# Layer 0's ramp in a two-layer encoder step: the second triangular inverse in other memory, the first read back behind its writing, fourteen products earlier

## The chip, the cores and the metric

The kernel runs on one core of a Trainium2 chip. The core has five engines with queues of their own: TensorE (PE, matrix products; its weight loads are listed as PEld), VectorE (DVE), ScalarE (ACT), GpSimd (POOL) and SyncE (SP, which here issues nearly every DMA). Semaphores order them against each other; within one engine, and within SP's DMA queue, work is issued in program order. The metric is the device time of one execution in microseconds (us), of which less is better.

## The reference

A streaming encoder trunk of two layers takes 512 prompt rows and 32 sample rows of width 1024. Each layer normalizes, projects once, runs a token mixer and a memory cross-attention, gates the result with SiLU, projects out and adds the residual. Layer 0's mixer is RWKV-7, a recurrence over a 64 x 64 state per head, 24 heads:

```python
def step(S, inp):
    r_t, k_t, v_t, w_t, kk_t, a_t = inp
    sa = jnp.einsum('bhvk,bhk->bhv', S, -kk_t)
    S = (S * w_t[:, :, None, :] + sa[..., None] * (kk_t * a_t)[:, :, None, :]
         + v_t[..., None] * k_t[:, :, None, :])
    return S, jnp.einsum('bhvk,bhk->bhv', S, r_t)
```

Layer 1's mixer is differential attention. Everything is float32.

## The kernel before

The 544 token rows lie as columns. A projection of 128 output columns is a *block* of 48 products: the weights are split into a high and a low part, and `ps_g` gathers, for each of 8 slices of the depth, high times `hh`, high times `hl` and low times `hh`, in two halves of 272 columns. `load` brings a block's weights in two pieces of 256 KB (`raw`, five buffers); ACT casts each to `whi` and DVE makes `wlo`, once for each piece. `stream` loads the weights of a block two blocks ahead and puts the casts off to places between products (`some`).

The recurrence is done in chunks of 64 tokens, for two heads (a *pair*) at once; there are 12 pairs. For a pair, `rw_prep` (a generator, taken a step at a time) makes decayed keys and the chunks' triangular matrices `at` and, for the sample rows, `ats`. The diagonal 32 x 32 blocks have to be inverted:

- at its end `rw_prep` writes these blocks to a DRAM scratch `sc1` (`sc<-at`, `sc<-ats` in the profile, which leaves numbers out of names);
- `rw_invert` ("inv") reads the scratch into `m3` three times, so that 102 partitions hold 34 blocks and three column classes, sets `u3` to the identity `ui` and does 31 steps of two POOL instructions (`tm`, `u`);
- `rw_back` ("back") writes `u3` to a second scratch `sc2`, and `rw_at` ("at") reads that back into `at` and `ats`;
- `rw_merge` ("mrg") makes from the two inverted blocks of a 64 x 64 matrix its off-diagonal block: DVE transposes (`t1b`), PE multiplies (`ps_w1`), ACT copies (`wm`), PE multiplies (`ps_w2`), ACT copies into `at`. In the profile both products are `ps_w`.

`m3` and `u3` have one buffer each, so an inverse can begin only when the one before has been written out. Then `rw_values` ("val") makes `ps_v`, and `rw_chain` takes the state through eight chunks in 23 hops between PE, ACT and DVE (`ps_c`, `sv`, `SB`, `avz`).

The order of every engine's work in layer 0 is fixed by the program: `go(kind, pair)` emits a step and `fill(n)` emits n products of the stream. The ramp (lines 1395 to 1426) takes pair 0's preparation with `FILL0`, pair 1's with `FILL1`, eleven steps of pair 2's with `FILL2`, and pair 0's merge and values with `FILL3`. In the ramp "back 0" stands ahead of `FILL2`'s loop, and "at 0" and "inv 1" at its fourth place:

```python
go("back", 0)
for k, n in enumerate(FILL2):
    go("prep", 2)
    if k == 2:
        go("rsq", 2)
    if k == 3:
        go("at", 0)
        go("inv", 1)
    fill(n)
```

Then the main loop takes, for each pair, the 23 chain hops with a table `PLAN` of steps for other pairs between them; `each[pr]` products are spread over the hops by their due times (144 for pair 0). The step `load_up`, in `rw_prep`, loads `up` for the pair after when DVE's `uz` has used the one before. `sg`, two tiles of 544 columns, hold gates from pair 1's loop on. `gsq` is a tile for squares in `rw_finish`, first used in pair 1's loop.

Of the kernel before, what the change touches and what calls it, by code (L numbers as in the profile page):

```python
# [9 lines left out]
F32 = mybir.dt.float32  # L10
# [7 lines left out]
P = 128  # L18
# [4 lines left out]
T = TP + TS  # L23
TH = T // 2
MIXW = 1536
NPAIR = MIXW // P
# [12 lines left out]
SGB = 2  # L39
# [38 lines left out]

FILL0 = [4, 4, 8, 2, 6, 2, 2, 2, 6, 2, 18, 4, 4, 2, 2, 0, 8, 12, 4, 8, 14, 10, 6, 14, 2, 0, 2, 2, 2, 2, 2, 2]
FILL1 = [6, 14, 12, 2, 4, 2, 2, 2, 8, 0, 10, 0, 2, 8, 8, 6, 4, 6, 6, 8, 18, 12, 8, 10, 0, 0, 0, 0, 4]  # L80
FILL2 = [4, 6, 12, 2, 2, 0, 4, 0, 6, 2, 2]
FILL3 = [16, 0, 2, 6]

OUT_ORDER = [0, 1, 2, 3, 4, 5, 6, 7, 8, 9, 10, 12, 13, 14, 15, 11]
# [3 lines left out]
NCL = 3  # L88
NBLK = 34
# [16 lines left out]
class Trunk:  # L106
# [600 lines left out]
    def rw_invert(self, st):  # L707

        nc, p, sc1 = self.nc, self.rb, st["sc1"]
        m3 = p.tile([NCL * NBLK, 32, 32], F32, tag="m3", name="m3", bufs=1)  # L710
        for q in range(NCL):
            self.se.dma_start(m3[q * 32 : q * 32 + 32], sc1[:32])
            self.se.dma_start(m3[96 + 2 * q : 98 + 2 * q], sc1[32:])
        st["u3"] = u3 = p.tile([NCL * NBLK, self.nr, 32], F32, tag="u3", name="u3", bufs=1)
        nc.gpsimd.tensor_copy(u3[:], self.ui[:])
        tm = p.tile([NCL * NBLK, self.nr, 32], F32, tag="tm", name="tm", bufs=1)
        for kx in range(31):
            n = kx // NCL + 1
            wd = 31 - kx
            sh = [NCL * NBLK, n, wd]  # L720
            nc.gpsimd.tensor_tensor(tm[:, :n, :wd], u3[:, :n, kx : kx + 1].to_broadcast(sh),  # L721
                                    m3[:, kx : kx + 1, kx + 1 :].to_broadcast(sh), ALU.mult)
            nc.gpsimd.tensor_tensor(u3[:, :n, kx + 1 :], u3[:, :n, kx + 1 :], tm[:, :n, :wd], ALU.add)  # L723

    def rw_back(self, st):

        u3 = st["u3"]
        st["sc2"] = sc2 = self.dp.tile([NBLK, 32, 32], F32, tag="sc2", name="sc2", bufs=2)
        for q in range(NCL):
            n = len(range(q, 32, NCL))  # L730
            for b, o, m in ((0, q * 32, 32), (32, 96 + 2 * q, 2)):
                self.se.dma_start(sc2[b : b + m, q : 32 : NCL, :], u3[o : o + m, :n, :])

    def rw_at(self, st):

        at, ats, sc2 = st["at"], st["ats"], st["sc2"]
        for e in range(2):
            o = 64 if e == 0 else 0
            for b in range(2):
                n = (e * 2 + b) * 8  # L740
                u = slice(o + 32 * b, o + 32 * b + 32)
                self.se.dma_start(at[u, e, 1 - e].rearrange("p i h t -> p (i h) t")[:, :, 32 * b : 32 * b + 32],
                                  sc2[n : n + 8].rearrange("b s t -> s b t"))
        self.se.dma_start(ats[64:96, 1, :, :32], sc2[32:34].rearrange("h s t -> s h t"))

    def rw_merge(self, st):

# [508 lines left out]
    def layer0(self, mem):  # L1256
        nc, o = self.nc, self.o
# [5 lines left out]
        with ExitStack() as ctx:  # L1263
# [23 lines left out]
            def go(kind, pr):  # L1287

                if kind == "rsq":
                    self.rsqrt(self.r20[:], self.q20[:], self.rk0, "nt20")  # L1290
                elif 0 <= pr < NPAIR:
                    if kind in ("inv", "back", "at"):
                        {"inv": self.rw_invert, "back": self.rw_back, "at": self.rw_at}[kind](sts[pr])
                        return
                    if (kind, pr) not in run:
                        it = run[kind, pr] = self.rw_prep(sts[pr], rkv[pr]) if kind == "prep" else make[kind](sts[pr])
                        next(it)
                    next(run[kind, pr], None)


            blocks, each = [], [0] * NPAIR
# [84 lines left out]
            def fill(n, each=6):  # L1386

                while n > 0:
                    for _ in range(min(n, each)):
                        next(main)  # L1390
                    n -= each
                    self.some(LATER)
# [20 lines left out]
                nc.gpsimd.memset(t[:, 4, :], 0.0)  # L1413
            self.pads(self.zr[2])
            self.at.append(self.rb2.tile([P, 2, 2, 4, 2, 64], F32, name="at2"))
            go("back", 0)
            for k, n in enumerate(FILL2):
                go("prep", 2)
                if k == 2:
                    go("rsq", 2)  # L1420
                if k == 3:
                    go("at", 0)
                    go("inv", 1)
                fill(n)
            for kind, n in zip(("mrg", "mrg", "val", "mrg"), FILL3):
                go(kind, 0)
                fill(n)
            for pr in range(NPAIR):
                mplan = MPLAN.get(pr, ())
                took = [HOP + sum(us for x in y for kind, d, us, _ in x if 0 <= pr + d < NPAIR) for y in PLAN]  # L1430
                load = [HOPV[k % 3] + sum(us for x in y for kind, d, _, us in x if 0 <= pr + d < NPAIR) for k, y in enumerate(PLAN)]
                whole = sum(took) + MEMPE * len(mplan) / 12 + MAIN * each[pr]

                pace = [max(x, 1.4) for x in load] if each[pr] < 3 * 6 * KT else [1.0] * len(PLAN)
                due = [whole * sum(pace[:k]) / sum(pace) for k in range(len(PLAN) + 1)]
                room = (sum(load) + 2.3 * each[pr] / 48) / len(PLAN)
                t, left, spent = 0.0, each[pr], 0.0
                for k, y in enumerate(PLAN):
                    go("chain", pr)
                    t += HOP  # L1440
                    spent += HOPV[k % 3]
                    for half, x in enumerate(y):
                        for kind, d, us, vus in x:
                            if 0 <= pr + d < NPAIR and kind != "full":
                                go(kind, pr + d)
                                t += us
                                spent += vus
                        for at, h in mplan:
                            if at == k + half / 2:
                                if h not in mit:  # L1450
                                    mit[h] = self.mem_steps(mems[h], 0, h, self.ma)
                                    next(mit[h])
                                next(mit[h], None)
                                t += MEMPE / 12
                        if FULL not in x:
                            spent += self.some(room * (k + (half + 1) / 2) + 0.4 - spent)
                        while left and t + MAIN / 2 < (due[k + 1] if half else (due[k] + due[k + 1]) / 2):
                            next(main)
                            t += MAIN
                            left -= 1  # L1460
# [27 lines left out]
        with ExitStack() as ctx:  # L1488
            p = self.pool("wo0", 1, ctx=ctx)
# [64 lines left out]
            pr = [self.psc.tile([P, 512], F32, tag="c", name="ps_r") for _ in range(2)]  # L1554
            for i in range(5):
                n = P if i < 4 else TS
# [4 lines left out]
            for k in range(KT):  # L1561
                h = p.tile([P, T], F32, tag="hn", name="hn", bufs=HNB)
# [253 lines left out]
    def run(self):  # L1816
# [9 lines left out]
        nc = self.nc  # L1826
# [5 lines left out]
        self.hl = hp.tile([P, KT, T], F32R, name="hl")  # L1832
        self.wp = self.pool("w", 1)
        gp = self.pool("gate", 1)
        self.sg, self.gates = [gp.tile([P, T], F32, name=f"sg{i}") for i in range(SGB)], 0
        self.rctx = ExitStack()
        self.rb = self.pool("rwb", 1, ctx=self.rctx)
        self.zr = [self.rb.tile([P, ZW], F32, name=f"zr{i}") for i in range(2)]
# [49 lines left out]
```

## Time and profile before

| What | Value |
|---|---|
| Median of three runs | 1451.4 us (1451.32 to 1452.59) |
| The profiled execution | 1452.73 us, span 1451.0 us |
| Mean granted clock of TensorE | 0.986 |
| PE, DVE, ACT, POOL busy | 96%, 63%, 58%, 27% of the span |
| DMA | 139.2 MB, mean 96 GB/s |

A timeline row gives a start and a duration in us, the engine, the line, the operation and its tiles, and in brackets how long the engine was idle before it and what ended that. Rows of equal instructions are merged, with their count. Nearly all work goes through a helper at line 103, so rows are told apart by their tiles. SPq rows are DMA issues and not landings. A table of stretches gives, for each, the busy time of the engines with the number of instructions, the granted clock as a share of full speed, the DMA engines' busy share and GB/s.

### The profile page before, as it was taken

Reading aid. Unit: us, or ns where it says so; the run is one execution under the profiler, and the core shown is the slowest. Engines: PE = TensorE matmul, PEld = TensorE weight load, DVE = VectorE, ACT = ScalarE, POOL = GpSimd, SP = SyncE. Lnnn points to the kernel's source line nnn. Section 1 sums busy time; section 2 is a strip of 40 time slices with the busy share of each in tenths; the row PEclk is TensorE's granted clock in tenths of the full one; section 3 lists DMA queues with packets and bytes.
Section 4 is the critical chain, followed back from the end, with each engine's and each line's share of the span. In section 5 each row is a group of like instructions: output and inputs, shape, how many; then the busy total and the mean of one; then the engine's idle time right before and its main releaser. Section 6 shows DMA issues by size and latency. Waiting matters only on the chain.

```text
span 1451.0 us, 31979 instructions
## 1 busy us (share of the span) xinstructions
PE 1397.4 (96%) x11906; PEld 1318.0 (91%) x11906; DVE 919.9 (63%) x2337; ACT 835.6 (58%) x2293; POOL 388.2 (27%) x846
## 2 busy tenths in 40 slices
PE   6998899999999999899999999999999999999997
PEld 5997899999999998788899999999999999999997
DVE  6565667787777887575743566664465745657533
ACT  6664667667776777455543366653565546664322
POOL 2025676566866567500120030000000001000200
PEclk9998999999999999999999999999999999999999
DMA  6442123323223222232554473323323222332321
GB/s 217 124 135 73 27 62 92 81 73 78 63 78 96 69 73 66 77 91 84 174 157 131 132 201 103 84 75 92 113 69 95 80 84 81 89 98 67 97 88 70
DMA packets 266533, 139.20 MB, mean 96 GB/s; under 512 B 57657, under 2 KB 256578, under 8 KB 266378
## 3 DMA queue, kind: packets, MB, share of 16 engines
q1 hardware_dynamic: 266378, 137.16, 33.4%
q8 instruction: 94, 1.54, 0.5%
q14 instruction: 61, 0.50, 0.1%
HBM read 110.98 MB, written 22.78 MB: 92 GB/s over the span
## 4 chain that ended last, share of the span: by engine, by line
PE 80%; DVE 7%; ACT 6%; issue 2%; POOL 2%; DMA 2%; SPq 1%; DVEq 0%; ACTq 0%; POOLq 0%
PE ps_g L103 57%; PE ps_c L103 4%; PE ps_s L103 2%; PE ps_o L103 2%; PE ps_at L103 2%; PE ps_mm L103 1%; PE ps_v L103 1%; DVE wlo L103 1%; PE ps_mo L103 1%; SPq L103 1%; PE ps_aT L103 1%; POOL u L723 1%; PE ps_ss L103 1%; PE ps_yc L103 1%; POOL tm L721 1%
## 5 line engine op out<-in xcount | busy, mean ns | idle before, releaser
L103 PE MATMUL ps_g<-hh,wlo 128*128 128x272 f32 x1808 | 539.5, 298 | 1.4 <-DVE wlo L103 1.4
L103 PE MATMUL ps_g<-hh,whi 128*128 128x272 f32 x1808 | 538.8, 298 | 0.0
L103 PE MATMUL ps_g<-hl,whi 128*128 128x272 f32 x1808 | 533.5, 295 | 0.0
L103 DVE TENSOR_TENSOR wlo<-raw,whi 128x512 fp32r<-128x512 f32 x322 | 224.1, 709 | 199.7 <-ACT whi L103 195.7
L103 PEld LDWEIGHTS ps_g<-hh,wlo 128*128 128x128 f32 x1808 | 342.8, 190 | 5.8 <-DVE wlo L103 2.0
L103 PEld LDWEIGHTS ps_g<-hh,whi 128*128 128x128 f32 x1808 | 343.6, 190 | 4.1
L103 PEld LDWEIGHTS ps_g<-hl,whi 128*128 128x128 f32 x1808 | 343.2, 190 | 3.9 <-issue 0.6
L103 ACT CAST whi<-raw 128x512 fp32r<-128x512 f32 x322 | 195.0, 617 | 180.5 <-PE ps_g L103 103.6
L721 POOL TENSOR_TENSOR tm<-u,m 102x84 f32<-102x84 f32 (+23 forms) x372 | 158.0, 425 | 181.1 <-DMA m<-sc 152.9
L723 POOL TENSOR_TENSOR u<-u,tm 102x84 f32<-102x84 f32 (+23 forms) x372 | 159.4, 429 | 29.1
L103 PE MATMUL ps_g<-lo,whi 128*128 128x272 f32 x512 | 148.6, 290 | 2.1 <-DVE lo L103 1.9
L103 PE MATMUL ps_g<-hi,whi 128*128 128x272 f32 x512 | 149.5, 292 | 0.8 <-ACT hi L103 0.8
L103 PE MATMUL ps_g<-hi,wlo 128*128 128x272 f32 x512 | 148.7, 290 | 0.9 <-DVE wlo L103 0.9
L1162 POOL TENSOR_TENSOR lo<-og,hi 128x544 fp32r<-128x544 f32 x8 | 13.7, 1713 | 485.8 <-DVE og L103 350.6
L103 PEld LDWEIGHTS ps_g<-lo,whi 128*128 128x128 f32 x512 | 97.2, 190 | 2.9 <-DVE lo L103 2.4
L103 PEld LDWEIGHTS ps_g<-hi,whi 128*128 128x128 f32 x512 | 97.2, 190 | 1.0 <-ACT hi L103 1.0
L103 PEld LDWEIGHTS ps_g<-hi,wlo 128*128 128x128 f32 x512 | 97.1, 190 | 1.1 <-DVE wlo L103 1.1
L103 DVE SCALAR_TENSOR_TENSOR SB<-ps_c,dl,sd 64x64 f32<-64x64 f32 x168 | 47.4, 282 | 47.4 <-PE ps_c L103 42.1
L103 ACT COPY sv<-ps_c 64x64 f32<-64x64 f32 x192 | 39.3, 205 | 39.0 <-PE ps_c L103 37.2
L103 ACT ACTIVATE pt<-ps_s,snm 128x128 f32<-128x128 f32 (+3 forms) x96 | 50.7, 529 | 18.1 <-DVE snm L103 17.0
L103 ACT ACTIVATE sg<-ps_g 128x272 f32<-128x272 f32 x64 | 25.3, 395 | 59.8 <-PE ps_g L103 59.5
L103 ACT COPY raw<-ps_g 128x272 f32<-128x272 f32 x74 | 28.6, 386 | 32.5 <-PE ps_g L103 31.8
(366 smaller groups left out, 2600.6 us busy)
## 6 DMA issues: line engine op xcount, KB each, us to landing
raw<-in_rw_in_dram SPq DMA_DIRECT2D x114, 256.0 KB
raw<-in_df_in_dram SPq DMA_DIRECT2D x112, 256.0 KB
raw<-in_w_out_dram SPq DMA_DIRECT2D x64, 256.0 KB
m<-sc SPq DMA_DIRECT2D x36, 128.0 KB
oscr<-sg SPq DMA_DIRECT2D x16, 272.0 KB
lo<-oscr SPq DMA_DIRECT2D x16, 272.0 KB
raw<-in_w_mem_k_dram SPq DMA_DIRECT2D x16, 256.0 KB
raw<-in_w_mem_v_dram SPq DMA_DIRECT2D x16, 256.0 KB
```

The lines of the kernel that those rows point to most:

```text
L103: return lambda *a, **k: self.trunk.tie(self, issue(*a, **k))
L721: nc.gpsimd.tensor_tensor(tm[:, :n, :wd], u3[:, :n, kx : kx + 1].to_broadcast(sh), m3[:, kx : kx + 1, kx + 1 :].to_broadcast(sh), ALU.mult)
L723: nc.gpsimd.tensor_tensor(u3[:, :n, kx + 1 :], u3[:, :n, kx + 1 :], tm[:, :n, :wd], ALU.add)
L1162: (self.nc.gpsimd if g % 2 else self.ve).tensor_tensor(lo[:], t, hi[:].bitcast(F32), ALU.subtract)
```

## The change

- Pair 1's inverse (and no other) takes its input into the gates' memory, which is now one tile `sg2` of which `sg[0]` and `sg[1]` are halves, and its result into `gsq`'s tile (`u3r`). It shares no buffer but `tm` with pair 0's inverse.
- "inv 1", "back 0" and "at 0" now stand together, in this order, at the third place of `FILL2`'s loop. "back 0" so moves behind the load of `up` and behind inverse 1's reads on SP, and two weight pieces move from ahead of "at 0" to behind it.
- `sc2` becomes two scratch tiles, of 32 and of 2 blocks, for all pairs; `rw_back` writes the three pieces of the large one first, and each read in `rw_at` waits only for its own tile.
- `FILL2` has 13 entries instead of 11 and 54 products instead of 40. Two steps of pair 2's preparation go with them out of pair 0's part of the main loop, which has 130 products instead of 144.

```diff
-FILL2 = [4, 6, 12, 2, 2, 0, 4, 0, 6, 2, 2]
+FILL2 = [4, 6, 12, 2, 2, 0, 4, 0, 6, 2, 6, 4, 6]
...
     def rw_invert(self, st):
...
-        m3 = p.tile([NCL * NBLK, 32, 32], F32, tag="m3", name="m3", bufs=1)
+        if st["pr"] == 1:
+            m3 = self.sg2[: NCL * NBLK, :1024].rearrange("p (s t) -> p s t", t=32)
+            u3 = self.rk0.tile([P, 10, 64], F32, tag="gsq", name="u3r", bufs=1)
+            u3 = u3[: NCL * NBLK].rearrange("p a b -> p (a b)")[:, : self.nr * 32].rearrange("p (n t) -> p n t", t=32)
+        else:
+            m3 = p.tile([NCL * NBLK, 32, 32], F32, tag="m3", name="m3", bufs=1)[:]
+            u3 = p.tile([NCL * NBLK, self.nr, 32], F32, tag="u3", name="u3", bufs=1)[:]
...
     def rw_back(self, st):
...
-        st["sc2"] = sc2 = self.dp.tile([NBLK, 32, 32], F32, tag="sc2", name="sc2", bufs=2)
-        for q in range(NCL):
-            n = len(range(q, 32, NCL))
-            for b, o, m in ((0, q * 32, 32), (32, 96 + 2 * q, 2)):
-                self.se.dma_start(sc2[b : b + m, q : 32 : NCL, :], u3[o : o + m, :n, :])
+        st["sc2"] = [self.dp.tile([m, 32, 32], F32, tag=f"sc2{m}", name=f"sc2{m}", bufs=2) for m in (32, 2)]
+        for o, t in zip((0, 96), st["sc2"]):
+            m = t.shape[0]
+            for q in range(NCL):
+                n = len(range(q, 32, NCL))
+                self.se.dma_start(t[:, q : 32 : NCL, :], u3[o + q * m : o + q * m + m, :n, :])
...
-            go("back", 0)
             for k, n in enumerate(FILL2):
                 go("prep", 2)
                 if k == 2:
                     go("rsq", 2)
-                if k == 3:
+                    go("inv", 1)
+                    go("back", 0)
                     go("at", 0)
-                    go("inv", 1)
                 fill(n)
...
+            ready = len(FILL2) - 11
+            each[0] -= sum(map(sum, (FILL0, FILL1, FILL2, FILL3))) - 4 * 24 - 6 * 48
...
-                            if 0 <= pr + d < NPAIR and kind != "full":
+                            if kind == "prep" and pr == 0 and d == 2 and ready:
+                                ready -= 1
+                            elif 0 <= pr + d < NPAIR and kind != "full":
...
-        self.sg, self.gates = [gp.tile([P, T], F32, name=f"sg{i}") for i in range(SGB)], 0
+        self.sg2, self.gates = gp.tile([P, SGB * T], F32, name="sg2"), 0
+        self.sg = [self.sg2[:, i * T : i * T + T] for i in range(SGB)]
```

SP's queue after pair 1's blocks have been written to `sc1`, before (the last two writes of inverse 0, then `up`, weights, the read-back, and the first reads of inverse 1):

```order
L103 DMA sc2_1783<-u3_1265 32x10x32
L103 DMA sc2_1783<-u3_1265 2x10x32
L103 DMA up_1800<-in_rw_w_up_dram 64x128 x2
L103 DMA up_1800<-in_rw_a_up_dram 64x128 x2
L103 DMA raw_1840<-in_rw_in_dram 128x4x128
L103 DMA raw_1842<-in_rw_in_dram 128x4x128
L103 DMA at0_90<-sc2_1783 32x8x32 x4
L103 DMA ats_1232<-sc2_1783 32x2x32
L103 DMA m3_1862<-sc1_1740 32x1024
L103 DMA m3_1862<-sc1_1740 2x1024
```

The same place now, from the last reads of inverse 1 on (`up` and the four reads before them stand directly ahead):

```order
L103 DMA sg2_83<-sc1_1739 32x1024
L103 DMA sg2_83<-sc1_1739 2x1024
L103 DMA sc232_1892<-u3_1258 32x11x32 x2
L103 DMA sc232_1892<-u3_1258 32x10x32
L103 DMA sc22_1893<-u3_1258 2x11x32 x2
L103 DMA sc22_1893<-u3_1258 2x10x32
L103 DMA at0_89<-sc232_1892 32x8x32 x4
L103 DMA ats_1231<-sc22_1893 32x2x32
L103 DMA raw_1916<-in_rw_in_dram 128x4x128
L103 DMA raw_1918<-in_rw_in_dram 128x4x128
```

Inverse 1's reads and `up` have moved ahead of the writes of inverse 0, and the weights `raw` behind the read-back.

ACT's queue at the merge of pair 0, before (`raw01` is a projection's result, `wm` and `at0` the merge's copies, `avz` the values'):

```order
L103 COPY raw01_351<-ps_g_1846 128x272
L103 COPY wm_2017<-ps_w1_2000 32x256 x2
L103 COPY avz_94<-ps_v0_2020 64x2x128
L103 COPY at0_90<-ps_w2_2028 32x8x32 x2
L103 COPY raw01_351<-ps_g_1983 128x272
```

and now:

```order
L103 COPY raw01_350<-PC_257 128x1
L103 COPY wm_2049<-ps_w1_2032 32x256 x2
L103 COPY avz_93<-ps_v0_2052 64x2x128
L103 CAST whi_2019<-raw_1916 128x512
L103 COPY at0_89<-ps_w2_2062 32x8x32 x2
```

The second half of the projection's result is now copied ahead of the merge, and the cast of the first of the two weight pieces that SP loads behind the read-back stands ahead of the copy into `at0`. On PE the first `ps_w1` comes 15 rows later, behind 14 products and pair 2's `ps_rt`; from pair 1's loop on, every engine's order is as before.

More of the change, by code (lines that the diff above doesn't have):

```diff
@@ L709, in rw_invert @@
         nc, p, sc1 = self.nc, self.rb, st["sc1"]
-        m3 = p.tile([NCL * NBLK, 32, 32], F32, tag="m3", name="m3", bufs=1)
+        if st["pr"] == 1:
[5 more added lines that the diff above has]
+            u3 = p.tile([NCL * NBLK, self.nr, 32], F32, tag="u3", name="u3", bufs=1)[:]
+        st["u3"] = u3
         for q in range(NCL):
@@ L713, in rw_invert @@
             self.se.dma_start(m3[96 + 2 * q : 98 + 2 * q], sc1[32:])
-        st["u3"] = u3 = p.tile([NCL * NBLK, self.nr, 32], F32, tag="u3", name="u3", bufs=1)
-        nc.gpsimd.tensor_copy(u3[:], self.ui[:])
+        nc.gpsimd.tensor_copy(u3, self.ui[:])
         tm = p.tile([NCL * NBLK, self.nr, 32], F32, tag="tm", name="tm", bufs=1)
@@ L742, in rw_at @@
                 self.se.dma_start(at[u, e, 1 - e].rearrange("p i h t -> p (i h) t")[:, :, 32 * b : 32 * b + 32],
-                                  sc2[n : n + 8].rearrange("b s t -> s b t"))
-        self.se.dma_start(ats[64:96, 1, :, :32], sc2[32:34].rearrange("h s t -> s h t"))
+                                  sc2[0][n : n + 8].rearrange("b s t -> s b t"))
+        self.se.dma_start(ats[64:96, 1, :, :32], sc2[1].rearrange("h s t -> s h t"))
     def rw_merge(self, st):
```

## The prediction

> **What bounds the kernel now.** I read the page first, then the stretches around the start of layer 0's main loop, then the timelines of five engines there.
>
> From the page, the busy time:
>
> ```profile
> PE 1397.4 (96%) x11906; PEld 1318.0 (91%) x11906; DVE 919.9 (63%) x2337; ACT 835.6 (58%) x2293; POOL 388.2 (27%) x846
> ```
>
> TensorE is busy 96% of the span, so a change pays only where PE waits or runs slowly. The table by stretches of the ramp (us, then busy time of PE, PEld, DVE, ACT, POOL, then granted clock, DMA share, GB/s):
>
> ```profile
> 135.00:139.00 4.00, 0.28 (x3) 0.17 (x2) 0.63 (x2) 0.09 (x1) 0.00 (x0) 0.78 0.82 196
> 139.00:147.00 8.00, 7.84 (x110) 6.92 (x109) 1.00 (x4) 3.85 (x12) 4.36 (x15) 0.50 0.48 139
> 147.00:160.00 13.00, 12.22 (x105) 11.63 (x103) 10.32 (x25) 9.43 (x25) 11.20 (x24) 0.98 0.08 21
> 160.00:177.00 17.00, 16.16 (x129) 14.78 (x130) 11.58 (x29) 11.13 (x34) 9.59 (x26) 1.00 0.11 18
> 177.00:181.00 4.00, 1.63 (x33) 1.30 (x34) 2.38 (x6) 0.05 (x1) 0.00 (x0) 0.65 0.36 74
> 181.00:186.00 5.00, 5.00 (x36) 4.94 (x32) 1.93 (x11) 2.62 (x9) 1.71 (x7) 0.60 0.63 186
> ```
>
> Two holes stand out, 135 to 139 and 177 to 181, each followed by a stretch in which the clock is halved. They are the merges of pairs 0 and 1. PE's and DVE's timelines name what ended them (start, duration, engine):
>
> ```profile
> 132.20 0.29 PE L103 MATMUL ps_g<-hh,whi 128*128 128x272 f32 x1
> ...
> 134.83 0.29 PE L103 MATMUL ps_g<-hh,whi 128*128 128x272 f32 x1
> 138.84 0.31 PE L103 MATMUL ps_w<-t1b,at 32*32 32x32 f32 x2 [3.72 <-DVE t1b L103]
> 139.30 1.06 PE L103 MATMUL ps_w<-t1b,at 32*32 32x32 f32 x30 [0.15 <-DVE t1b L103]
> 145.16 1.97 PE L103 MATMUL ps_v<-sv,at 64*64 64x64 f32 x28
> 177.22 0.38 PE L103 MATMUL ps_c<-SB,zr 128*128 128x128 f32 x2
> 179.37 0.31 PE L103 MATMUL ps_w<-t1b,at 32*32 32x32 f32 x2 [1.76 <-DVE t1b L103]
> 180.28 1.06 PE L103 MATMUL ps_w<-t1b,at 32*32 32x32 f32 x30 [0.61 <-DVE t1b L103]
> 187.47 0.69 PE L103 MATMUL ps_w<-at,wm 32*32 32x32 f32 x32
> ```
>
> ```profile
> 125.67 0.74 DVE L103 TENSOR_TENSOR uz<-up,uh 64x128 fp32r<-64x128 f32 x2 [1.44 <-ACT uh L103]
> 138.34 0.90 DVE L103 STREAM_TRANSPOSE t1b<-at 32x256 f32<-32x256 f32 x2 [3.83 <-DMA at<-sc]
> 179.80 0.43 DVE L103 STREAM_TRANSPOSE t1b<-at 32x256 f32<-32x256 f32 x1 [0.48 <-DMA at<-sc]
> ```
>
> Both times DVE's transposition waits for the read-back `at<-sc` of the inverse. PE idles 3.72 + 0.15 = 3.87 us for pair 0 and 1.76 + 0.61 = 2.37 us for pair 1. Behind the read-backs stand POOL's inverses and SP's in-order queue:
>
> ```profile
> 97.56 0.24 POOL L721 TENSOR_TENSOR tm<-u,m 102x31 f32<-102x31 f32 x1 [56.23 <-DMA m<-sc]
> 128.62 0.23 POOL L723 TENSOR_TENSOR u<-u,tm 102x11 f32<-102x11 f32 x1
> 132.12 1.56 POOL L715 CAST u<-ui 102x352 f32<-102x352 bf16 x1 [3.28 <-DMA sc<-u]
> 141.55 0.24 POOL L721 TENSOR_TENSOR tm<-u,m 102x31 f32<-102x31 f32 x1 [7.86 <-DMA m<-sc]
> 170.28 0.23 POOL L723 TENSOR_TENSOR u<-u,tm 102x11 f32<-102x11 f32 x1
> ```
>
> ```profile
> 122.80 0.39 SPq L103 DMA_DIRECT2D sc<-ats  x1
> 128.87 2.12 SPq L103 DMA_DIRECT2D sc<-u  x6
> 131.10 1.11 SPq L103 DMA_DIRECT2D up<-in_rw_w_up_dram  x2
> 132.25 1.23 SPq L103 DMA_DIRECT2D up<-in_rw_a_up_dram  x2
> 133.53 1.14 SPq L103 DMA_DIRECT2D raw<-in_rw_in_dram  x2
> 134.71 1.98 SPq L103 DMA_DIRECT2D at<-sc  x4
> 137.23 2.14 SPq L103 DMA_DIRECT2D m<-sc  x6
> 177.03 1.78 SPq L103 DMA_DIRECT2D at<-sc  x4
> ```
>
> The first inverse ends at 128.85, but its read-back is issued only at 134.71, behind four `up` loads and two weight loads, and lands at 138.3. The second inverse has its input in DRAM from about 125 on, yet starts at 141.55: its buffers are the first one's, and its reads stand behind the read-back. POOL idles 12.7 us between them.
>
> **The change, part by part.** Times are of the profiled execution (span 1451.0, its time 1452.7).
>
> *Second inverse begun at once.* SP now issues, behind pair 1's `sc<-ats`: `up` x4, the six reads of `sc1` into the gate memory, the six writes of the first inverse, the read-back. `up` waits for `uz`, which ends at 126.4; four issues take 1.11 + 1.23, with gaps 2.4 us, so the reads are issued from 128.9 to 131.0 (2.14 us). Their landing: POOL began 141.55 − 139.37 = 2.2 us after the last issue. So the second inverse starts at 133.2, 8.3 us earlier; its cast of `ui` no longer waits, as its `u` tile is another one. Its length is 29.0 us (141.55 to 170.51) or the first one's 31.3 us (97.56 to 128.85); I take 29.4, near the row of the same inverse, since it runs beside the same work of DVE, a few us sooner. It ends at 162.6. From its end to the last transposition's start is 179.80 − 170.51 = 9.3 us, six writes, pair 2's five scratch writes and the read-back, whose order stays; then 0.48 to PE. **PE can merge pair 1 at 172.4, not 180.28: 7.9 us earlier.**
>
> *First read-back right behind its writing.* The six writes are now behind `up` and the reads: issued 131.0 to 133.2, 2.2 us later than before; with the large three first, the read-back needs only these, issued by 132.1. Landing after the last issue was 132.12 − 130.99 = 1.1 us, so 133.3 at the earliest; with 0.4 MB of reads ahead on the same queue up to 134.9; I take 134.0. From the read-back's first issue to the last piece it took 179.80 − 177.03 = 2.8 us where nothing was ahead, 138.34 − 134.71 = 3.6 us behind two weight loads; the weight loads now follow, so 2.8: 136.8, and 0.45 for the second transposition: 137.3 instead of 139.24.
>
> *Fourteen products moved ahead of the merge.* A product is issued every 0.125 us (from 132.20 to 134.83, 21 issues). Fourteen take 1.75, and pair 2's `ps_rt`, which goes with them, 0.13: PE reaches the merge at 134.95 + 1.9 = 136.85. It waits 0.45 instead of 3.87. These products are gone from pair 0's loop, which has 130 instead of 144 between its 23 chain steps. That has a price: PE already idles 1.6 us of the 30 us in 147 to 177. Nothing to the whole 1.75 may come back as waits; I take 0.6, nearer the row, where chain steps are mostly covered.
>
> *The half clock behind the first merge.* From 139.30 to 147.1 PE works 7.8 us at 0.50. The same chain at full clock: two merges of 0.69 (the row at 187.47), two ACT copies between them of 0.74, 1.0 for the value products (half of 145.16's 1.97), and, as an estimate, 0.9 of chunk 0 and hand-overs: about 4.8. Three microseconds at most; nothing if the clock is halved all the same. One thing takes part of it: the weight loads `raw` are now behind the read-back, and ACT's cast of the first now stands ahead of the copy of the second merge's result:
>
> ```profile
> 140.39 0.74 ACT L103 COPY wm<-ps_w 32x256 f32<-32x256 f32 x2 [5.30 <-PE ps_w L103]
> 148.43 0.62 ACT L103 CAST whi<-raw 128x512 fp32r<-128x512 f32 x1
> ```
>
> That load is issued from 136.5 to 137.1 instead of at 133.53; with the 2.2 us of the inverse's reads it lands at 139.3. ACT is free for it at about 139.1, after `wm` and one copy more. Its cast of 0.62 and a wait of 0 to 1 us go on the path: I take 0.4 beyond what PE's six products cover. So pair 0's loop starts at 137.3 + 4.8 + 0.4 = 142.5 instead of 147.1. PE then reaches pair 1's merge (before at 177.22 + 0.38 = 177.6) 4.6 + 1.9 − 0.6 = 5.9 us earlier, at 171.7. That is ahead of the inverse's 172.4: **the inverse sets the time there, gain 7.9**, and PE waits 0.7 instead of 2.37.
>
> *The half clock behind the second merge.* PE ran at 0.50 from 178.24 to 185.07. From 180.28 on this cost about 1.9 us (4.8 us, not all of it bound by the clock). Whether it comes back is shown by rows of stretches of 3.41 us each:
>
> ```profile
> 133.87:137.28 3.41, 1.24 (x10) 1.02 (x9) 0.65 (x2) 1.19 (x3) 0.00 (x0) 1.00 0.75 188
> 174.83:178.24 3.41, 2.42 (x19) 2.04 (x17) 2.00 (x6) 2.17 (x6) 0.14 (x1) 1.00 0.21 32
> 181.65:185.07 3.42, 3.42 (x17) 3.42 (x17) 1.04 (x6) 2.19 (x8) 0.98 (x5) 0.50 0.71 212
> 270.40:273.81 3.41, 3.35 (x53) 2.95 (x52) 2.31 (x7) 2.46 (x8) 1.26 (x2) 1.00 0.34 101
> 273.81:277.23 3.42, 3.42 (x16) 3.42 (x16) 3.15 (x11) 2.01 (x8) 2.79 (x9) 0.50 0.57 162
> ```
>
> The clock falls at ends of such stretches (137.28, 178.24, 273.81) when the stretch held little streaming: at 270.40 PE was 3.35 of 3.41 busy, with small matmuls (`ps_ss`, `ps_w`), and was halved all the same. Pair 1's merge keeps its `ps_ss` and 0.7 us of waiting, so a stretch that falls badly is still halved, at 1.7 us at most (half of 3.41). I take half of the 1.9, 1.0.
>
> The Trainium skill, page "TensorE: Matmul & The Clock Gate", Part 1, says that the gate judges free-running windows of 3413 ns, and in its part on oscillation that idle gaps above about 3.4 us are what to avoid. The windows agree with this trace: some 10 us at half from 137.28 (0.50 in 139 to 147, 0.98 from 147), and 40.96 us, twelve windows, from there to 178.24. The rule on gaps does not: at 178.24 the gap was only 0.6 us old. By that rule both merges would now stay at full clock and the sum would be 9.8; by the rows it is 8.9.
>
> *Hidden or free:* splitting `sc2` leaves the bytes and the twelve issues per pair as they are; both halves of `sg2` are tracked apart, and the first gate's write needs the second inverse done, 25 us before pair 1's gate; `u3r` is read out some 45 us before the square that uses that tile (pair 0's is in pair 1's loop). `SS0` and the next weights on SP move with the queue, ahead of where they are needed by 10 us or more (the cast at 148.43 came 14.9 us after its load was issued). SP then waits for the second inverse as before, but 8 us earlier. Pair 2's inverse, whose reads follow pair 1's read-back, also starts some 9 us earlier; in the whole span the transposition waited for a read-back only at these two pairs (us in total, times, longest):
>
> ```profile
> DVE t1b L103 <- DMA at<-sc: 5.4, 3, 3.8
> ```
>
> So nothing behind pair 1 is paced by it, and the 96% busy TensorE carries the gain to the end.
>
> **Sum.** 7.9 + 1.0 = 8.9 us. Against its own time 1452.7 − 8.9 = 1443.8; that execution was 1.3 above the median of 1451.4, so the forecast is 1442.5.
>
> **Rivals.**
> 1. *Both merges at full clock* (the page's rule, as worked out above from 178.24 to 185.07): 0.9 more, 1441.6. For it: the long hole is gone. Against: the row at 270.40.
> 2. *The read-back comes late*, held by 0.4 MB of reads ahead of it: issued at 134.9, 3.6 to land, transposed at 139.0. PE then waits 2.1 us at pair 0 and the clock is halved again there (2 us): the loop starts at 139.0 + 5.2 + 2 = 146.2, PE reaches pair 1 at 177.6 − 0.9 − 1.9 + 0.6 = 175.4, later than the inverse. The gain there is 4.9, and with the second halving unchanged the time 1446.5. For it: the DMA share of 0.82 in 135 to 139. Against: no weight load is ahead of the read-back any more.
> 3. *The clock takes it back.* All work after the ramp comes some 8 us earlier against the 3.41 us grid, so which later stretches fall under is drawn anew. Three more halved ones at 1.7 us, in the loops of the later pairs, leave 7.9 − 5.1 = 2.8 us: 1448.6, within 0.2% (2.9 us, about what a measurement of this kernel can tell from no change). For it: the row at 270.40, whose work recurs with every pair. Against: that row is one pair's; the two rows of halving at the merges stood beside idle time.
> 4. *Slower:* pair 0's loop is bound by its chain, not by products. Its 23 steps would have to wait 0.39 us more each to eat 8.9; above that it ends slower, at 0.6 us each 1451.4 − 8.9 + 13.8 = 1456.3. Against: the idle shown there is 1.6 us over some 17 steps, 0.1 each, and removing 14 of 144 products takes 0.08 us of cover from a step.
>
> **How the numbers follow.** Forecast 0.42, rival 1 0.25, rival 2 0.19, rival 3 0.07, rival 4 0.07. Low end: rival 1 with the inverse at 29.0 and the reads landing 0.5 earlier, 1440.5. High end: rival 2's 1446.5 with half a microsecond more, 1447.0; that leaves out rivals 3 and 4 (0.14) and some of the tails. Faster by over 0.2% holds the first three and a part of rival 3: 0.87; within 0.2%, 0.06; slower, 0.07.
>
> **What would show it.** POOL's second inverse starting at 132.5 to 134 with no wait for a write of `u`; the read-back of pair 0 issued 133.3 to 135; the transposition's wait for `at<-sc` under 2 us in all; clock at or near 1.00 in 139 to 147; PE's first merge at 137 to 138, its second at 171.5 to 174; pairs 2 to 11 shifted alike. Wrong would be: ACT waiting for a `raw` over 1 us before the copy into `at`, PE idle over 3 us in pair 0's loop, or a DVE wait for a read-back at a later pair.

## The result, and the profile after

The changed kernel takes 1445.35 us (median of seven runs, 1443.89 to 1447.31); the kernel before, run beside it, 1452.59. The ratio is 0.9951 with a 95% interval of 0.9939 to 0.9964: 7.1 us faster, 5.2 to 8.9. The forecast was 1442.5 in a range of 1440.5 to 1447.0, from a gain of 8.9.

The table by stretches shows where the time went. Both kernels are cut at the same work: from 126 to the first merge's 30 small products, to the second merge's, to the end of pair 0's loop (its first `ps_yc`) and of pair 1's. Behind the stretch's length stand the busy times of PE, PEld, DVE, ACT and POOL, then the clock, the DMA share and GB/s. Before:

```profile
126.00:139.30 13.30, 8.87 (x67) 8.19 (x67) 6.79 (x22) 6.63 (x16) 3.78 (x10) 0.92 0.38 85
139.30:180.28 40.98, 36.99 (x344) 33.91 (x344) 24.28 (x58) 24.47 (x71) 25.14 (x63) 0.87 0.18 44
180.28:190.38 10.10, 10.10 (x114) 9.36 (x114) 4.72 (x17) 6.27 (x20) 5.43 (x16) 0.76 0.58 167
190.38:236.97 46.59, 46.06 (x466) 42.96 (x465) 37.04 (x90) 33.67 (x97) 30.32 (x67) 1.00 0.26 65
```

After:

```profile
126.00:137.49 11.49, 10.86 (x81) 10.05 (x82) 6.49 (x21) 7.61 (x20) 5.37 (x20) 1.00 0.32 73
137.49:172.68 35.19, 32.47 (x333) 29.59 (x333) 24.89 (x58) 23.76 (x69) 21.69 (x53) 1.00 0.25 60
172.68:181.86 9.18, 9.09 (x111) 8.34 (x111) 4.14 (x16) 5.90 (x19) 4.78 (x14) 0.81 0.63 183
181.86:228.05 46.19, 45.67 (x467) 42.86 (x466) 36.83 (x90) 33.64 (x97) 29.76 (x67) 1.00 0.26 66
```

Pair 1's loop ends 8.9 us earlier (236.97 to 228.05). PE's idle time up to there, length less busy time, fell from 9.0 to 4.0 us. The time at half clock (twice the missing share of the clock, times the length) fell from 17.6 to 3.5 us. The other 3.9 of the gain are put down to that: less than half of the 14.1 us taken away, as not all work takes twice as long at half clock (the 30 small products of the first merge took 1.06 us there and 0.69 at full clock). 0.2 us of the 3.9 stood already at 126, where the table begins.

The timelines show the three steps. POOL, with the end of inverse 0, the start of inverse 1 and its last instruction:

```profile
128.69 0.23 POOL L729 TENSOR_TENSOR u<-u,tm 102x11 f32<-102x11 f32 x1
133.57 0.61 POOL L727 TENSOR_TENSOR tm<-u3r,sg 102x31 f32<-102x31 f32 x1 [4.65 <-DMA sc<-u]
162.87 0.23 POOL L729 TENSOR_TENSOR u3r<-u3r,tm 102x11 f32<-102x11 f32 x1
```

SP's issues around the two read-backs:

```profile
129.40 2.18 SPq L103 DMA_DIRECT2D sg<-sc  x6
131.67 2.34 SPq L103 DMA_DIRECT2D sc<-u  x6
134.36 1.78 SPq L103 DMA_DIRECT2D at<-sc  x4
...
163.12 2.35 SPq L103 DMA_DIRECT2D sc<-u3r  x6
...
169.15 1.91 SPq L103 DMA_DIRECT2D at<-sc  x4
```

DVE at the first merge, then at the second:

```profile
136.13 0.44 DVE L103 STREAM_TRANSPOSE t1b<-at 32x256 f32<-32x256 f32 x1 [1.87 <-DMA at<-sc]
137.00 0.43 DVE L103 STREAM_TRANSPOSE t1b<-at 32x256 f32<-32x256 f32 x1 [0.44 <-DMA at<-sc]
...
170.81 0.17 DVE L103 TENSOR_SCALAR q<-ps_ss 128x10 f32<-128x10 f32 x1 [1.17 <-PE ps_ss L103]
171.01 0.69 DVE L103 TENSOR_TENSOR wlo<-raw,whi 128x512 fp32r<-128x512 f32 x1
171.73 0.90 DVE L103 STREAM_TRANSPOSE t1b<-at 32x256 f32<-32x256 f32 x2
```

PE at both:

```profile
137.08 0.24 PE L103 MATMUL ps_w<-t1b,at 32*32 32x32 f32 x2
137.49 0.69 PE L103 MATMUL ps_w<-t1b,at 32*32 32x32 f32 x30 [0.17 <-DVE t1b L103]
...
171.09 0.38 PE L103 MATMUL ps_c<-SB,zr 128*128 128x128 f32 x2
172.22 0.24 PE L103 MATMUL ps_w<-t1b,at 32*32 32x32 f32 x2 [0.75 <-DVE t1b L103]
172.68 0.69 PE L103 MATMUL ps_w<-t1b,at 32*32 32x32 f32 x30 [0.22 <-DVE t1b L103]
```

At the second merge DVE no longer waits for the read-back: its transposition follows `wlo` and `q<-ps_ss` without a gap. PE's 0.75 us are those of DVE's queue. POOL's row for the start of inverse 1 names a write of `u` (`sc<-u`) as what ended the wait, but `early_reads` below shows that inverse 1 needs none of these writes.

Of the 8.9 us, 7.5 reach the end of the span. The lead had grown to 10.1 us at the end of pair 2's loop, as the stretch from 273.81 that is halved in the kernel before has no counterpart here. It was 9.6 at the end of pair 5's loop and 8.5 at that of pair 6's, in which the clock is halved for one stretch that was not halved before, and 7.9 at the end of pair 11's. The rows show two of the halved stretches, at the second merge and in pair 6's loop, each behind the stretch ahead of it:

```profile
169.85:173.26 3.41, 2.44 (x46) 2.14 (x45) 2.26 (x7) 0.94 (x2) 0.00 (x0) 1.00 0.39 82
173.26:176.67 3.41, 3.41 (x21) 3.37 (x16) 1.19 (x7) 2.08 (x7) 0.51 (x3) 0.50 0.65 192
446.33:449.74 3.41, 3.34 (x52) 3.06 (x53) 2.65 (x8) 2.43 (x7) 1.86 (x5) 1.00 0.14 37
449.74:453.15 3.41, 3.41 (x17) 3.41 (x16) 3.05 (x10) 2.38 (x9) 2.81 (x8) 0.50 0.57 168
```

### The profile page after: what moved, and what is told of

The parts are those of the page before. It is cut to its first block, busy times and chain, and to the rows that moved or that the text cites. A ratio compares the mean times of both kernels' runs of the same rounds, so it can differ in the third digit from the quotient of the medians.

```text
span 1443.5 us, 31980 instructions
## 1 busy us (share of the span) xinstructions
PE 1393.5 (97%) x11906; PEld 1314.4 (91%) x11906; DVE 921.6 (64%) x2337; ACT 836.8 (58%) x2293; POOL 386.8 (27%) x846
## 4 chain that ended last, share of the span: by engine, by line
PE 84%; ACT 6%; DVE 6%; issue 2%; DMA 2%; SPq 1%; DVEq 0%; ACTq 0%
PE ps_g L103 58%; PE ps_c L103 5%; PE ps_o L103 2%; PE ps_s L103 2%; PE ps_at L103 2%; PE ps_v L103 1%; PE ps_mm L103 1%; SPq L103 1%; PE ps_mo L103 1%; PE ps_aT L103 1%; PE ps_ss L103 1%; PE ps_yc L103 1%; DVE wlo L103 1%; PE ps_w L103 1%; ACT whi L103 1%
## 5 line engine op out<-in xcount | busy, mean ns | idle before, releaser
L727 POOL TENSOR_TENSOR tm<-u,m 102x84 f32<-102x84 f32 (+23 forms) x341 | 142.9, 419 | 177.1 <-DMA m<-sc 151.4
L729 POOL TENSOR_TENSOR u<-u,tm 102x84 f32<-102x84 f32 (+23 forms) x341 | 150.1, 440 | 26.6
```

## The experiments

Each kernel is compared with the kernel before, run beside it on the same chip (its median there 1450.8 to 1451.8); "4.2 us under" is the ratio's distance from 1 times that median, with its 95% interval.

Places in a trace are those of one execution. Already at pair 1's scratch writes on SP (`sc<-at`), ahead of everything that the edits move in that queue, the executions stand up to 1.3 us apart: 120.88 in the kernel before, 120.66 with the change, 119.72 to 121.01 in all. So differences of places of about a microsecond prove little.

### Parts alone and undone

Theory A is the prediction's: the start of inverse 1 sets when pair 1 can be merged. Its rival B: the hole and the half clock at the first merge were the loss, and the 14 products are the gain.

*Without the products* (`no_products`):

```diff
-FILL2 = [4, 6, 12, 2, 2, 0, 4, 0, 6, 2, 6, 4, 6]
+FILL2 = [4, 6, 12, 2, 2, 0, 4, 0, 6, 2, 2]
```

> The change with FILL2 as before: the 14 products and pair 2's two steps stay in pair 0's loop. Theory A (the second inverse's start sets when pair 1 can be merged, and with it the end): inverse 1 starts at 133.6 as with the whole change; PE reaches the first merge near 135, waits some 2.3 us for the read-back, and reaches pair 1's merge 1 to 3 us later than 172.2; 4 to 6.5 us under the kernel before, where the whole change was 7.1 under it. Theory B (the hole at the first merge and the half clock behind it were the loss, and the 14 products are the gain): at most 2 us under the kernel before.

4.2 us under the kernel before (2.8 to 5.8; 1447.61 us). PE waits 1.36 and 0.65 us at the first merge, the clock is halved for two stretches behind it, and the second merge stands at 175.69, 3.0 later than with the whole change, behind PE's own work. By the ratios the products are worth about 3 us, though the two intervals overlap a little (0.9960 to 0.9981 here, 0.9939 to 0.9964 for the change), and only beside the rest of the change, as the next run shows.

*The products alone* (`products_only`): the long `FILL2`, `ready` and the line on `each` in the kernel before.

> The kernel before with the long FILL2 alone: memory, scratch and order of the inverses as before. Theory A: inverse 1 starts near 141.5 and pair 1's merge stands at 180 as before; PE has done 14 products more by then and waits for the read-back 4 to 7 us instead of 2.4; time 0 to 1.5 us under the kernel before. Theory B: 3.5 to 5 us under it.

0.6 us under (0.9 over to 2.0 under; 1451.19). Inverse 1 starts at 140.64. PE waits 1.09 us for `t1b` at the first merge where it was 3.72, and longer at the second instead:

```profile
138.32 0.69 PE L103 MATMUL ps_w<-t1b,at 32*32 32x32 f32 x30 [0.15 <-DVE t1b L103]
178.15 0.31 PE L103 MATMUL ps_w<-t1b,at 32*32 32x32 f32 x2 [3.66 <-DVE t1b L103]
179.04 1.06 PE L103 MATMUL ps_w<-t1b,at 32*32 32x32 f32 x30 [0.57 <-DVE t1b L103]
```

*The steps in their old order* (`old_order`): other memory, scratch and products stay.

```diff
+go("back", 0)
 for k, n in enumerate(FILL2):
...
-        go("inv", 1)
-        go("back", 0)
-        go("at", 0)
+    if k == 3:
+        go("at", 0)
+        go("inv", 1)
```

> The whole change, but back 0 again ahead of FILL2's loop and at 0, inv 1 at its fourth place. Theory A: the reads of inverse 1 stand behind the read-back on SP again, so inverse 1 starts at 140 to 141.6 although its memory is free, and pair 1's merge stands at 178.5 to 180; 0 to 2 us under the kernel before. Rival (the other memory by itself frees the inverse, the order is worth little): inverse 1 starts by 137 and the time is 4 us or more under the kernel before.

No difference from the kernel before (1.5 under to 1.3 over; 1452.18). Inverse 1 has its own memory and still starts late, since its reads stand behind the read-back on SP:

```profile
141.34 0.76 POOL L727 TENSOR_TENSOR tm<-u3r,sg 102x31 f32<-102x31 f32 x1 [9.30 <-DMA sg<-sc]
```

PE idles 6.63 us at the second merge. Memory without order gains nothing that can be measured; both together move the inverse.

*The half clock taken away and nothing else* (`before_filled`): idle products into the holes of the kernel before.

```diff
         ps = self.psx.tile([P, 512], F32, tag="x", name="ps_w1")
+        for _ in range({0: 20, 1: 30}.get(st["pr"], 0)):
+            self.te.matmul(ps[:, :TH], self.hh[:, 0, :P], self.hh[:, 0, :TH], start=True, stop=True)
```

> The kernel before with idle products (hh times hh, 0.125 us each) on PE ahead of ps_w1: 20 (2.5 us) in the hole of 3.87 us at pair 0's merge and 30 (3.75 us) at pair 1's; the real products write over their result, nothing else changes. It takes away the half clock and leaves both waits for the inverses. Theory A (inverse 1 sets pair 1's merge, the clock decides the rest): first merge at 139 and second at 180 as before, pair 0's loop up to 3 us shorter at full clock and as much more waiting at pair 1's merge; only the stretch behind the second merge gains, 1 to 2.5 us under the kernel before. Rival (the half clock was the loss, the wait for inverse 1 little): 3.5 us or more under it, pair 1's merge near 177.

1450.98 beside 1450.93 us, ratio 1.0003 (0.9994 to 1.0012): no difference, less than theory A's 1 to 2.5. The clock is full through both merges:

```profile
126.00:139.70 13.70, 11.31 (x87) 10.66 (x87) 6.52 (x21) 6.36 (x16) 3.45 (x11) 1.00 0.36 83
139.70:178.98 39.28, 37.27 (x372) 34.47 (x372) 24.07 (x57) 24.46 (x71) 25.00 (x63) 1.00 0.19 46
178.98:187.16 8.18, 8.18 (x117) 7.45 (x117) 4.81 (x18) 6.28 (x20) 3.58 (x10) 1.00 0.57 161
187.16:234.61 47.45, 45.88 (x467) 42.94 (x466) 36.79 (x90) 33.59 (x97) 30.36 (x71) 1.00 0.27 70
```

In this execution pair 1's loop ends 2.4 us earlier than before (234.61 against 236.97), and the 8.18 us behind the second merge answer to 10.10. The medians do not show it; this one execution took 1449.95 us and the profiled one of the kernel before 1452.73, and in this round the kernel before ranged from 1449.15 to 1452.75. So B is out as far as the medians reach, to 1 or 2 us: the half clock is taken away here and most of the hole in `products_only`, and neither gained. With inverse 1 at 141, what is saved at the first merge is for the most part waited off at the second.

The second merge comes 1.3 us earlier here (178.98 against 180.28) although inverse 1 ends 0.5 later. From the inverse's end to the read-back's issue it is 5.0 us here and 6.5 in the kernel before, where one of SP's five writes for pair 2 in between takes 1.72 us to issue instead of some 0.45. No view names why.

### What sets the second merge now

*Inverse 1 later* (`late_inverse`, `later_inverse`): two and eight casts more on POOL.

```diff
         for kx in range(31):
+            if st["pr"] == 1 and kx == 1:
+                for _ in range(2):
+                    nc.gpsimd.tensor_copy(tm[:], self.ui[:])
```

> The whole change with two more casts of ui into tm (1.56 us each) on POOL behind the first step of inverse 1, so it ends 3.1 us later; tm is written over, so nothing else changes. Theory A: pair 1's merge moves by 2.4 to 3.1 us, and the time rises by as much, by up to 1.7 more if the longer hole halves the clock for one stretch more: 2.5 to 4.7 us under the kernel before. Rival (PE's own work sets pair 1's merge by now): at least 6.2 us under it, PE waiting in the place of a later idle spell.

5.1 us under (3.3 to 7.0; 1447.64). The dose was smaller than meant, 0.51 us for a cast and not 1.56:

```profile
134.44 1.02 POOL L726 CAST tm<-ui 102x352 f32<-102x352 bf16 x2
```

The inverse ended at 164.1, 1.0 later than with the change, and the merge came 0.8 later (173.46). By the ratios the time is 2.0 above the change, which the intervals do not separate (0.9952 to 0.9977 against 0.9939 to 0.9964); in this execution the clock was halved for two stretches at the second merge, with the change for one. Hence eight casts (`range(8)`):

> As late_inverse, with eight casts of ui into tm instead of two. There two casts took 1.02 us, so eight take 4.1. Theory A': with the change, the read-back of pair 1 lands about when DVE comes to transpose it; from there on every microsecond that inverse 1 ends later is one by which pair 1's merge and the end are later. Merge at 176.3 to 176.7 (172.7 with the change), PE waiting 4.5 to 5 us there; time 3.5 to 5.5 us above the change, 1.5 to 3.5 under the kernel before. Rival (later loops have room and take the delay up): less than 2.5 above the change.

1.9 us under (0.1 to 3.6; 1450.22), 5.2 above the change by the ratios. The inverse ended at 167.8, 4.7 later than with the change; the merge came 3.4 later (176.09), with PE waiting:

```profile
175.06 0.31 PE L103 MATMUL ps_w<-t1b,at 32*32 32x32 f32 x2 [4.90 <-DVE t1b L103]
176.09 1.06 PE L103 MATMUL ps_w<-t1b,at 32*32 32x32 f32 x30 [0.73 <-DVE t1b L103]
```

So inverse 1 has about a microsecond to spare, and one that is later by more is paid for. The next run asks whether an earlier one would help.

*Inverse 1 earlier* (`early_reads`):

```diff
+go("inv", 1)
 for k, n in enumerate(FILL2):
...
-        go("inv", 1)
         go("back", 0)
```

> The change with inv 1 ahead of FILL2's loop, so that SP issues inverse 1's reads ahead of up and inverse 1 begins when inverse 0 ends: at 129.5 to 130.5 instead of 133.6. Theory A' (at pair 1's merge the read-back and DVE's own queue, wlo behind q<-ps_ss, now end together; an earlier inverse finds DVE no earlier): merge 1 stays within 0.5 us of 172.7, and the time within 0.2% of the change's, 6 to 8 us under the kernel before. Rival (the inverse's end still sets pair 1's merge alone, as the prediction had it): merge 1 earlier by 0.7, all that PE waits there, with 1.3 for the halved stretch behind it: 9 us under the kernel before.

9.3 us under (7.3 to 11.2; 1442.89 us, 1441.99 to 1444.12); the theory's 8 and the rival's 9 both lie in that interval. Inverse 1 starts at 127.31, 6.3 earlier than with the change and earlier than either theory had it, since inverse 0 ends 1.8 us earlier in this execution. It starts ahead of the writes of `u`, so it does not need them. It ends at 158.7. The second merge moves by only 1.4 us, and with the same two waits:

```profile
127.31 0.24 POOL L727 TENSOR_TENSOR tm<-u3r,sg 102x31 f32<-102x31 f32 x1 [0.18 <-DMA sg<-sc]
128.75 2.54 SPq L103 DMA_DIRECT2D sc<-u  x6
...
136.39 0.69 PE L103 MATMUL ps_w<-t1b,at 32*32 32x32 f32 x32
...
170.78 0.24 PE L103 MATMUL ps_w<-t1b,at 32*32 32x32 f32 x2 [0.75 <-DVE t1b L103]
171.25 0.69 PE L103 MATMUL ps_w<-t1b,at 32*32 32x32 f32 x30 [0.22 <-DVE t1b L103]
```

Of those 1.4 us, 1.1 stand already at the first merge (136.39 against 137.49), and 0.7 of them ahead of the edit (`sc<-at` at 119.94 against 120.66). SP issues pair 0's read-back at 131.64 instead of 134.36, because inverse 1's reads moved ahead of `up`, but that earns little: in `later_inverse`, whose `sc<-at` also stands at 119.94 and whose read-back is issued at 133.23, the first merge comes at 136.34. From the first merge to the second PE needs 34.9 us, with the change 35.2. So with the change PE's own way from the first merge, hand-overs to ACT and DVE included, sets the second, and inverse 1 is just in time. Both theories had the place of the inverse wrong, and the rival had the wait wrong too: it stayed.

*Weights ahead of the read-back* (`weights_first`):

```diff
-        go("at", 0)
+    if k == 3:
+        go("at", 0)
```

> The change, but the two weight pieces stand ahead of the read-back on SP (at 0 at the fourth place of FILL2's loop, back 0 and inv 1 at the third). Theory by the prediction: the read-back is issued 1.1 us later, at 135.5, and lands 0.8 later behind the weights; PE waits 1.8 to 2.4 us at the first merge instead of 0.6, ACT's cast no longer waits 0.56; merge 1 is 0.5 to 1.5 us later, the clock may halve behind the first merge for up to 1.7 more: 0.5 to 3 above the change, 4 to 6.5 under the kernel before. Rival (the read-back's place does not matter, since inverse 1 sets pair 1's merge): within 0.5 of the change.

3.6 us under (2.2 to 5.1; 1447.85), 3.5 above the change by the ratios. The first merge is 1.05 later, in an execution that was 0.9 ahead at `sc<-at`, and PE waits 1.99 us there:

```profile
137.58 0.90 DVE L103 STREAM_TRANSPOSE t1b<-at 32x256 f32<-32x256 f32 x2 [4.27 <-DMA at<-sc]
```

The clock is halved for two stretches behind it, and the second merge is 3.4 later (176.03). This is rival 2 of the prediction, made on purpose: it was priced at 4.0 above the forecast.

*One scratch again* (`one_scratch`): `rw_back` and `rw_at` as before, in the new order.

> The change with one scratch of 34 blocks per pair, written in the old order of large and small pieces, so that the first read of the read-back waits for all six writes and not for three. Theory D (since PE's own way from the first merge sets the second, each microsecond of pair 0's read-back counts): read-back 0.4 to 1.1 us later than 134.4, PE waits as much more at the first merge, merge 1 later by as much; 0.4 to 1.1 us above the change, up to 1.7 more if the first merge is halved by it: 4.3 to 6.7 under the kernel before. Rival (inverse 1 sets merge 1): within 0.3 us of the change.

6.7 us under (4.8 to 8.7; 1444.44): no difference from the change. SP waits 0.97 us between the last write and the read-back (with the change 0.35), so the split is worth 0.6 us there by the two traces; the times cannot show that.

### What is left

*The 14 products out of pair 1's loop instead* (`full_loop`):

```diff
-            each[0] -= sum(
+            each[1] -= sum(
```

> The change, but pair 0's loop keeps its 144 products: the 14 that the ramp took come out of pair 1's loop. Theory C (the thinned loop costs more than the 0.6 us of the prediction: PE idles 2 us in 160 to 174): the products fill that idle time, 1 to 2.5 us under the change, 8 to 9.5 under the kernel before. Rival (PE reaches merge 1 later by what it does more, 1.75 us, and waits less there): within 0.5 us of the change, as in no_products, where the loop had the same 144.

4.2 us under (2.6 to 5.9; 1448.0), 2.9 worse than the change by the ratios (0.9959 to 0.9982 against 0.9939 to 0.9964), where I had expected it better.

```profile
136.76:172.86 36.10, 33.65 (x344) 30.95 (x344) 25.07 (x58) 23.55 (x69) 21.07 (x53) 1.00 0.28 70
172.86:184.14 11.28, 10.85 (x114) 10.07 (x114) 5.50 (x18) 7.50 (x24) 6.40 (x15) 0.71 0.50 136
184.14:230.75 46.61, 43.72 (x453) 41.19 (x452) 35.57 (x88) 31.61 (x91) 29.43 (x70) 1.00 0.24 61
```

Pair 0's loop with all its products idles 2.45 us against 2.72 without the 14: thinning it costs 0.3. Pair 1's loop, thinned by the same 14, idles 2.89 us against 0.52. In this execution the clock is also halved for two stretches at the second merge instead of one, and from there to the end of pair 0's loop it takes 11.28 us against 9.18. How much of the 2.9 is the clock's and how much the loop's stays open.

*The second merge filled* (`filled_merge`): the two lines of `before_filled` in the changed kernel, with six products for pair 1 alone.

> The change with six idle products (hh times hh, 272 columns, 0.125 us each) on PE ahead of pair 1's ps_w1, in the 0.75 us in which PE waits for the transposition; the real products write over their result, so only PE has more to do. Theory E (the clock goes by how much is streamed in a stretch of 3.41 us): the stretch ahead of 173.3 is fuller by 0.75 us, the halving behind it goes away in most executions; merge 1 at 172.5 to 173, time 0.7 to 1.7 us under the change, 8 to 9 under the kernel before. Rival (0.75 us is too little, or the halving there comes from elsewhere): halved as before, time 0 to 0.5 above the change.

5.1 us under (3.0 to 7.0; 1446.32): not faster than the change. At the second merge the clock stays full; behind the first it is halved in this execution, which it was not with the change:

```profile
137.40:140.81 3.41, 3.07 (x79) 2.66 (x79) 1.22 (x2) 2.43 (x6) 2.86 (x8) 1.00 0.76 202
140.81:144.22 3.41, 3.41 (x35) 2.98 (x35) 0.84 (x1) 1.58 (x7) 2.79 (x9) 0.50 0.95 262
171.53:174.95 3.42, 3.20 (x51) 2.83 (x51) 2.48 (x8) 0.81 (x3) 0.00 (x0) 1.00 0.59 139
174.95:178.36 3.41, 3.41 (x30) 3.41 (x29) 1.61 (x9) 2.80 (x9) 1.40 (x6) 1.00 0.65 188
```

*The transposition earlier* (`early_transpose`): `early_reads`, and for pair 0's loop alone

```diff
+                    if pr == 0 and k in (15, 16):
+                        (a, b), m = y, ("mrg", 1, 0, 0.86)
+                        y = [a, [m] + b] if k == 15 else [a, [x for x in b if x != m]]
```

> early_reads, with DVE's transposition for pair 1's merge one hop earlier in pair 0's loop (and in no other pair's), ahead of uz, SB, q<-ps_ss and wlo. Theory F (PE's 0.75 and 0.22 us at pair 1's merge are DVE's queue and not the inverse, which ends ten microseconds earlier): PE no longer waits there, merge 1 at 170.1 to 170.5 instead of 171.25; 0.8 to 1.0 us under early_reads, 1 more where the halved stretch behind it goes too: 10 to 11.3 under the kernel before. Rival (the wait moves to the next hand-over, SB or avz behind the transposition): within 0.4 of early_reads.

9.1 us under (7.3 to 10.9; 1442.86): the same as `early_reads`. PE's wait for `t1b` at the second merge is gone, as theory F has it, the stretch behind it is not halved, and pair 0's loop ends at 177.96 instead of 180.46. By the end of pair 10's loop that lead is lost (645.01 against 644.72), with one stretch more at half clock near 448 and one near 600. `early_reads` is the best version measured together with this one; its interval overlaps that of the change (0.9923 to 0.9950 against 0.9939 to 0.9964), so that it beats the change is likely and not shown.

## Why the prediction was right, and where it was not

- *Second inverse begun at once.* Start 133.2 forecast, 133.57 measured; length 29.4, 29.5; end 162.6, 163.1; second merge 172.4, 172.68. The gain of 7.9 measured 7.6. `products_only` and `old_order` show that without it the rest gains nothing measurable.
- *From the inverse's end to the last transposition.* The 9.3 us were taken from one execution as fixed. Their first part, up to the read-back's issue, took 6.5 us there, 6.05 with the change and 5.0 in `before_filled` and `early_reads`. That the sum held here is in part luck.
- *First read-back.* Issued 134.0, measured 134.36; last transposition done 137.3, 137.43. PE's wait 0.45, measured 0.17.
- *Half clock behind the first merge.* Gone: 1.00 from 137.49 to 172.68; pair 0's loop starts at 142.46, 142.5 forecast. That this alone gains nothing measurable is shown by `before_filled`.
- *Thinned loop.* 0.6 forecast, 0.3 by the idle times of `full_loop` and the change. Rival 4, which needed 9 us of it, is out.
- *"The inverse sets the time there."* PE reached the second merge at 171.5 (171.7 forecast) and waited 0.75, as said, but for DVE's queue and not for the inverse. `early_reads` shows it. The number held since both ends fell within a microsecond, which is luck. The reading of what comes next did not hold: an earlier inverse finds PE no earlier, and what is paid for from here on is a later first merge (`weights_first`) or an inverse later by more than a microsecond (`later_inverse`). Where `early_reads` gets its 2.2 us, if they are real, stays open.
- *Half clock behind the second merge.* 1.0 forecast; from the merge to the end of pair 0's loop 10.10 became 9.18: 0.9. One stretch of the two was left, against rival 1.
- *The sum.* 8.9 forecast and 8.9 measured at the end of pair 1's loop. The two terms gave 8.5 of it (7.6 and 0.9); the other 0.4 came in pair 1's loop (46.19 against 46.59), for which the sum had no term, so the exact agreement is chance. The step that failed is the last one, that TensorE carries the gain to the end: 7.5 arrived in the profiled execution and 7.2 by the medians. That is rival 3's mechanism at a third of its size (1.7 of 5.1). The other 1.2 us of the 2.9 between forecast and median lie in the base: the kernel before ran at 1452.59 here and not at 1451.4.
- *The signs.* Two did not come. DVE waited 2.31 us in all for the read-back (1.87 and 0.44) and not under 2; PE, which had its own work meanwhile, paid 0.17 of that. And pairs 2 to 11 are not shifted alike: the lead falls from 10.1 to 7.9 us. The range's low end is 0.2 under what its own terms give (1441.6 less 0.4 and 0.5).

The Trainium skill, page "TensorE: Matmul & The Clock Gate", Part 1, names idle gaps above about 3.4 us as what to avoid. The stretch from 169.85 has none longer than 0.75 us and is followed by a halved one, as at 178.24 before; by the rule the sum would have been 9.8.

## What to carry to other kernels

Where two waits of one engine stand in a row, removing the first is worth nothing until the second can move too: each of the three edits that left inverse 1 where it was gained nothing that could be measured. Freeing a buffer starts nothing early while the transfer that fills it stands behind a waiting one in an in-order queue; look for what is ahead of it there. And when a wait has gone, read again what ended the one in its place: the profile named the same pair of tiles, but the engine between them was now waiting for something else.

## What the runs showed of the hardware

- The clock does not go by PE's busy share. It was halved after stretches of 3.41 us with PE busy 2.44, 3.07 and 3.34 us, and stayed full after one of 3.20 us, in which six products of 272 columns had taken the place of 0.75 us of waiting. With the change it also stayed full after one of only 2.31 us, from 582.86. Many small products (32 columns, or 2 for `ps_ss`) stood in the halved ones, but no run shows what counts.
- Which stretches are halved differs from execution to execution. Apart from the two merges and the time after TensorE's last product, the profiled executions had five such stretches before, five with the change and one with `early_reads`. Near 27 us, ahead of what the edits move, there were one, two and none. That blurs gains of one or two microseconds: two kernels whose profiled executions led by 2 to 3 us at the end of a loop (`before_filled`, `early_transpose`) show nothing in their medians.
- The same cast of 102 x 352 on POOL took 1.56 us in the kernel before, 0.90 and 0.48 in the same place in `before_filled` and `products_only`, and 0.51 in `late_inverse`, where two took 1.02. No run tells why; a dose should be measured and not taken from another place.
